# One core's decoder layer: eight modulation half-rows summed over the partitions by chained accumulating DMAs instead of by TensorE

## The chip, the core and the metric

The kernel runs on one core of one Trainium2 chip. The metric is the device time of one launch in microseconds (us), the median of three runs. TensorE is called PE, VectorE DVE, ScalarE ACT, GpSimd POOL and SyncE SP. POOL and SP each issue DMAs in the order of their own instruction stream; an instruction that waits holds up all that stands behind it on its engine.

## The reference, cut to what matters

One layer of a decoder on 512 tokens of width 1024, in float32. The modulation vectors come from one vector `c`:

```
cs  = silu(c)                                   # 1024
mod = cs @ w_ada + b_ada                        # 1024 x 6144
shift1, scale1, gate1, shift2, scale2, gate2 = split(mod, 6)
h    = rmsnorm(x, norm1_g) * (1 + scale1) + shift1
proj = h @ w_in                                 # queries, keys, values, gates ga and gd
merged = sigmoid(ga) * (swa(proj) @ w_branch_swa) + sigmoid(gd) * (diff(proj) @ w_branch_diff)
x  = x + gate1 * (merged @ w_out)
h2 = rmsnorm(x, norm2_g) * (1 + scale2) + shift2
x  = x + gate2 * conv_ffn(h2)
out = rmsnorm(x, final_g)
```

The change is about the last four of the six modulation vectors: gate1, shift2, scale2 and gate2. They are computed beside the two attentions and the merge, and are needed only after them.

## The kernel before, in words

Matrices are multiplied in float32 by splitting each operand into a high and a low half and adding three products (`mm3`: high x high, high x low, low x high); the halves of a weight are made by a cast on ACT and a subtraction on DVE (`split_pair`). Raw weights come over SP's queue into a ring of six buffers (`raw_tile`), so a load waits until the split that read its buffer is done.

From 57 us to 309 us PE runs through 288 steps of three 128x512 matmuls each: the projections of the four differential heads (`add_head`: pq, pk, pw), the gates of the windowed branch (`add_gate_a`: pga) with its branch product (pA), then the gates of the differential branch (`add_gate_d`: pgd) with theirs (`add_merge`: pB). Between the steps stand the small matmuls of the attentions. PE's order is the order in which the program is written: `fill(n)` emits n steps, and each call counts one tick. `after(n, fn)` has `fn` emitted n ticks later. The order on DVE, ACT, POOL and SP is set by a list scheduler with priorities; in the changed kernel POOL's order in this stretch, too, is the order of the program.

The four modulation vectors are 4 x 1024 numbers, kept as eight half-rows of 512 (named by vector and half: 00, 01, 10, 11, 20, 21, 30, 31). Every 8 ticks `ada_rows` loads 256 rows of `w_ada` for one half-row (tile `ra`) and DVE adds them, times `cs`, to a running sum of 128 partitions x 512 (tile `arow`); after four such turns, 32 ticks, the 128 partial sums of each of the 512 columns are ready. `ada_spread` then sums over the partitions: four float32 matmuls with a matrix of ones (tile `pr`), a copy on ACT to SBUF (tile `row`), and one DMA on POOL's queue into `mod_rows` in DRAM. Two running sums are alive at a time. Where `ada_spread` stands on PE is set by `flush("row")` at places written out by hand.

After the merge, gate1 is read back from `mod_rows` for all partitions (tile `g1b`) and multiplied into the rows of `w_out` (tile `wo`); shift2 and scale2 are read back as 16 x 128 (tile `m2`), and one transpose on PE (tile `pm2`) turns them for the second normalisation. Those reads stand on POOL's queue. POOL also takes the power -1/2 of the statistics of the differential heads (`rstd_start`, tile `r0`), for which DVE waits.

Of the kernel before, what the change touches and what calls it, by code (L numbers as in the profile page):

```python
# [11 lines left out]
ALU = mybir.AluOpType  # L12
# [45 lines left out]
def kernel(  # L58
# [52 lines left out]

    splits = []
# [376 lines left out]
    outa = [big.tile([P, 4, S], F32R, tag=f"out{g}", name=f"outa{g}") for g in "hl"]  # L489

    def evac(hi, lo, src, scale=None):
        if scale is None:
            nc.scalar.copy(hi, src)
            nc.vector.tensor_sub(lo, src, hi.bitcast(F32))
        else:
            nc.scalar.activation(hi, src, AF.Copy, scale=scale)
            return nc.vector.scalar_tensor_tensor(lo, src, scale, hi.bitcast(F32), ALU.mult, ALU.subtract)

# [33 lines left out]
    man = ExitStack()  # L532
    man.enter_context(tc.manual_schedule(engines={nc.tensor.engine}))
    units, loaded, later = [], [], []
    current, tick = [], [0]
# [30 lines left out]

    beside = {"row": [], "sum": [], "end": [], "norm": [], "turn": []}

    def after(n, fn):
        later.append([n, fn])  # L570
# [19 lines left out]
    def swa_scores(i, blocks):  # L590
# [26 lines left out]
        for n in blocks:  # L617
# [3 lines left out]
            for j in range(2):  # L621
                with tc.high_priority(offset=HP):
                    c.last = nc.vector.tensor_tensor_reduce(
                        c.sb[n][:, j, :w], sps[n // 2, j][:, n % 2, :w], dsw[:, 256 - w : 256], 1.0, -3e38, ALU.add, ALU.max,
                        c.mx[:, j, n : n + 1],
                    )

    def swa_softmax(i):
# [92 lines left out]

    maxima = []

    def diff_scores(*ss):
# [20 lines left out]
        for s, sps, w in ops:  # L745
# [3 lines left out]
            for m in range(2):  # L749
                st = ap.tile([P, w], F32, tag="st", bufs=ST, name=f"sd{h}_{n}_{m}")  # L750
                with tc.high_priority(offset=HP):
                    maxima.append(nc.vector.tensor_tensor_reduce(
                        st, sps[m], ddf[:, 512 - w : 512], 1.0, -3e38, ALU.add, ALU.max, mx[:, m : m + 1]
                    ))
# [4 lines left out]
    def diff_softmax(*ss):  # L759
        with tc.high_priority(offset=HP):  # L760
# [3 lines left out]
            for s in ss:  # L764
# [15 lines left out]
                behind.enter_context(tc.issue_after(last.ins))  # L780
            behind.close()

    def diff_transpose(s):
# [72 lines left out]
    def ada_rows():  # L856
# [5 lines left out]
        for (idx, hf, k), job in zip(todo, todo[ADA_AHEAD:] + [None] * ADA_AHEAD):  # L862
# [16 lines left out]
            if k == KT - 2:  # L879
                row = lambda idx=idx, hf=hf, ac=ac: ada_spread(idx, hf, ac)  # L880
                if group_ahead:
                    beside["row"].append(row)
                else:
                    after(ADA_LAG, row)
            yield

    spread = []


    def ada_spread(idx, hf, ac):  # L890
        pr = tbank(f"pr{idx}{hf}", (P, P))
        for g in range(4):
            gs = slice(32 * g, 32 * g + 32)
            nc.tensor.matmul(
                pr[gs], ones[:, gs], ac[:, g * P : (g + 1) * P], start=True, stop=True, tile_position=(0, 32 * g)
            )
        row = big.tile([P, P], F32, tag="g2b0", name=f"row{idx}{hf}")
        with tc.high_priority(offset=HP):
            spread.append(nc.scalar.copy(row, pr))  # L899
        nc.gpsimd.dma_start(  # L900
            mod_rows[idx, hf * S : (hf + 1) * S].rearrange("(g n) -> g n", g=4), row[0:P:32]
        )


    pair_w = {}

    def add_gate_a(j):
# [5 lines left out]
        def load():  # L913
            if j % 2 == 0:
# [6 lines left out]

                with tc.issue_after(spread[-1].ins) if j == 0 else ExitStack():
                    pair_w["a"] = split_pair(r, [P, 4, 2 * P], f"wba{j}")
            return pair_w["a"]

        def branch(wts):
            o = fbank(f"pA{j}")
            rhs = [[outa[b][:, k] for k in range(4)] for b in range(2)]
            yield from steps(o, wts, rhs, 4, cl=slice(j % 2 * P, j % 2 * P + P))
            nc.vector.scalar_tensor_tensor(ta[:, j], ta[:, j], 1.0, o, ALU.add, ALU.mult)  # L930

        units.append((lambda: load_cols(win, COL_GA + j * P, f"wga{j}"), gate))
        units.append((load, branch))

    group_ahead, sums = [1], {}
    pairs, firsts, scored, probs, aTs = {}, {}, {}, {}, {}
    ada = ada_rows()
    add_head(0)
    add_head(1)
    with tc.issue_after(last_mod.ins):  # L940
# [12 lines left out]
    for i in range(SWA_PAIRS):  # L953
        more = i + 1 < SWA_PAIRS
        fill(SWA_FILL[3])
        if more:
            flush("row")
            swa_scores(i + 1, range(NT))
# [10 lines left out]
        if i < 2:  # L969
            flush("row")  # L970
            swa_values(i)
        fill(SWA_FILL[7])
    while units or loaded or current:
        fill(1)
    flush("row")
    swa_values(2)
# [3 lines left out]
    ta = big.tile([P, KT, S], F32, tag="qa", name="ta")  # L980
    for j in range(2):
        add_gate_a(j)
    diff_scores(0, 1)
    diff_softmax(0, 1)
    fill(DIFF_FILL[0])
    for s in range(4 * DIFF_HEADS):
        h, n = divmod(s, NT)
        if s in (4, 8):
            add_head(h + 1)
        elif s == 12:  # L990
            add_gate_a(2)
            add_gate_a(3)
        ahead = s == 1
        fill(DIFF_FILL[1] - ahead)
        nxt = (s + 1, s + 2) if n % 2 and s < 15 else ()
        if nxt:
            flush("row")
            diff_scores(*nxt)
        if n == 3:
            with tc.issue_after(maxima[-1].ins):  # L1000
                flush("end")
# [7 lines left out]
        if n != 1:  # L1009
            diff_transpose(s)  # L1010
        if s == 13:
            group_ahead.clear()
        elif s > 13:
            flush("row")
        diff_softmax(*nxt)
        if n == 0 and h:
            diff_values(h - 1)
            fill(DIFF_FILL[3])
    for j in range(4, KT):
        add_gate_a(j)  # L1020
    fill(4)
    flush("norm")
    diff_values(DIFF_HEADS - 1)
    while units or loaded or current:
        fill(1)
# [16 lines left out]
    def add_gate_d(j):  # L1042
# [6 lines left out]
        units.append((lambda: load_cols(win, COL_GD + j * P, f"wgd{j}"), gate))  # L1049

    def add_merge(j):
        def load():
# [9 lines left out]
        def branch(wts):  # L1062
# [3 lines left out]
            td = tds[j]  # L1066
            nc.vector.scalar_tensor_tensor(td, td, 1.0, o, ALU.add, ALU.mult)
            nc.vector.tensor_add(td, td, ta[:, j])
            split(mgh[j], mgl[j], td)

        units.append((load, branch))

    for j in range(KT):
# [3 lines left out]
    add_merge(KT - 1)  # L1077
    while units or loaded or current or later:
        fill(1)
    for _ in ada:  # L1080
        fill(1)
    while later:
        fill(1)
    man.close()


    def brow(dst, src):
        nc.gpsimd.dma_start(dst, src.partition_broadcast(P))

# [8 lines left out]
    m2 = bp.tile([40, P], F32, name="m2")  # L1098
    nc.gpsimd.dma_start(m2[0:16, :], mod_rows[1:3].rearrange("r (a p) -> (r a) p", p=P))
    nc.gpsimd.dma_start(m2[16:32, :], b_ada[0, 3 * D : 5 * D].rearrange("(a p) -> a p", p=P))  # L1100
    nc.gpsimd.dma_start(m2[32:40, :], norm2_g[0].rearrange("(a p) -> a p", p=P))
    pm2 = tbank("pm2", (P, 40))
    nc.tensor.transpose(pm2, m2, ident[:40, :40])
    c2 = bp.tile([P, 40], F32, name="c2")
    nc.vector.tensor_copy(c2, pm2)
    nc.vector.tensor_add(c2[:, 0:16], c2[:, 0:16], c2[:, 16:32])
    s2c, a2c = c2[:, 0:8], c2[:, 8:16]
    nc.vector.scalar_tensor_tensor(a2c, a2c, 1.0, c2[:, 32:40], ALU.add, ALU.mult)
    nc.vector.tensor_scalar_mul(a2c, a2c, -0.5)

    x1 = big.tile([P, NT, D], F32, tag="qa", name="x1")
# [850 lines left out]
```

## Time and profile before

| | us |
|---|---|
| median of three runs | 691.83 (691.79 to 692.15) |
| the profiled execution | 692.45 |
| its span, first to last instruction | 690.5 |
| PE busy | 679.9 (98%) |
| DVE busy | 564.6 (82%) |
| ACT busy | 383.1 (55%) |
| POOL busy | 82.7 (12%) |

The granted clock of PE was 0.997 over the span. The span begins with the first normalisation and projection (to 57 us), goes on with the attentions and the merge (to 309 us), the product with `w_out` (to about 354 us), the gated MLP (to 683 us) and the last normalisation. Busy time of an engine does not count the issuing of DMAs, and idle time of an engine that nobody waits for costs nothing; so the table says little without the waits, which the prediction reads.

### The profile page before, as it was taken

The numbers are of one execution on the slowest core, as the hardware profiler recorded it, in microseconds if no ns is written. First come the engines' busy times: TensorE is split into PE (matmuls) and PEld (weight loads), VectorE is DVE, ScalarE is ACT, GpSimd is POOL, SyncE is SP. The second block draws the span as 40 slices with busy tenths as digits, with TensorE's granted clock in tenths as the row PEclk, the third lists the DMA queues.
The fourth block names the chain that finished last, engine by engine and source line by source line (L and its number), as shares of the span: only waits on it lengthen the run. The fifth ranks groups of instructions, "written<-read, shape, count | busy, mean of one in ns | idle before, by whom it ended". The sixth has DMA issues, their size and how long they took to land.

```text
span 690.5 us, 11249 instructions
## 1 busy us (share of the span) xinstructions
PE 679.9 (98%) x4203; PEld 592.7 (86%) x4203; DVE 564.6 (82%) x1073; ACT 383.1 (55%) x686; POOL 82.7 (12%) x100
## 2 busy tenths in 40 slices
PE   8999999999999999999999999999999999999995
PEld 5787877788888888888899999999999999888884
DVE  4889987878876775663589988888888999979997
ACT  6676775445542323332377756655555666656665
POOL 3000000000001000000030101112120002540300
PEclk9999999999999999999999999999999999999998
DMA  9995554444626882239635798777889747995903
GB/s 306 327 318 152 183 159 132 136 126 128 183 66 184 275 257 104 91 101 318 222 61 124 170 220 189 167 172 216 191 225 220 157 154 186 195 202 149 168 1 121
DMA packets 115926, 121.81 MB, mean 176 GB/s; under 512 B 4447, under 2 KB 93344, under 8 KB 115872
## 3 DMA queue, kind: packets, MB, share of 16 engines
q1 hardware_dynamic: 96958, 95.09, 43.7%
q0 software_dynamic: 18720, 25.73, 22.1%
q8 instruction: 33, 0.54, 0.3%
q10 hardware_dynamic: 194, 0.28, 0.1%
q14 instruction: 21, 0.17, 0.1%
HBM read 118.97 MB, written 2.11 MB: 175 GB/s over the span
## 4 chain that ended last, share of the span: by engine, by line
PE 95%; DMA 2%; DVE 1%; ACT 1%; issue 0%; SPq 0%; POOLq 0%; ACTq 0%
PE up L1291 32%; PE dc L1906 15%; PE a L388 3%; PE pga L125 2%; PE pgd L125 2%; PE oc L1347 2%; PE pga L127 2%; PE pga L126 2%; PE pgd L127 2%; PE oc L1351 2%; PE oc L1348 2%; PE pgd L126 2%; PE sd L132 1%; PE pq L125 1%; PE pw L125 1%; PE pA L125 1%
## 5 line engine op out<-in xcount | busy, mean ns | idle before, releaser
L1291 PE MATMUL up<-t,m_whi 128*128 128x256 f32 x512 | 93.1, 283 | 0.0
L1291 PEld LDWEIGHTS up<-t,m_whi 128*128 128x128 f32 x512 | 79.9, 192 | 0.0
L1291 PE MATMUL up<-t,m_wlo 128*128 128x256 f32 x256 | 72.5, 283 | 0.0
L1291 PE MATMUL up<-bl,p_whi 128*128 128x256 f32 x232 | 65.7, 283 | 0.0
L1291 PE MATMUL up<-bh,p_wlo 128*128 128x256 f32 x232 | 65.7, 283 | 0.0
L1291 PE MATMUL up<-bh,p_whi 128*128 128x256 f32 x232 | 65.7, 283 | 0.0
L1291 PEld LDWEIGHTS up<-t,m_wlo 128*128 128x128 f32 x256 | 49.2, 192 | 0.0
L878 DVE SCALAR_TENSOR_TENSOR arow<-ra,cs,arow 128x512 f32<-128x512 f32 x56 | 41.9, 748 | 8.1 <-DMA ra<-in_w_ada_dram 7.4
L1291 PEld LDWEIGHTS up<-bh,p_whi 128*128 128x128 f32 x232 | 44.5, 192 | 0.0
L1291 PEld LDWEIGHTS up<-bl,p_whi 128*128 128x128 f32 x232 | 44.5, 192 | 0.0
L1291 PEld LDWEIGHTS up<-bh,p_wlo 128*128 128x128 f32 x232 | 44.5, 192 | 0.0
L1200 POOL DMA_DIRECT2D s<-in_w_up_dram x21 | 27.0, 1362 | 140.5 <-DMA s<-in_w_up_dram 72.5
L1228 ACT CAST m_whi<-s 128x1024 fp32r<-128x1024 f32 x31 | 32.5, 1047 | 11.1 <-DVE s L1222 7.7
L1232 DVE TENSOR_TENSOR m_wlo<-s,m_whi 128x1024 fp32r<-128x1024 f32 x31 | 37.7, 1218 | 0.0
L1291 PE MATMUL up<-t,p_whi 128*128 128x256 f32 x176 | 32.2, 283 | 0.0
L188 POOL TENSOR_TENSOR r<-ms,mhalf 128x1 f32<-128x1 f32 (+1 forms) x16 | 13.1, 818 | 134.9 <-DVE ms L186 70.5
L900 POOL DMA_DIRECT2D mod_rows<-row x8 | 5.0, 630 | 194.2 <-ACT row L899 194.2
L1291 PEld LDWEIGHTS up<-t,p_whi 128*128 128x128 f32 x176 | 27.5, 192 | 0.0
L1298 ACT ACTIVATE gT<-a,cv 128x512 f32<-128x512 f32 x22 | 17.7, 813 | 16.9 <-DVE a L1333 15.8
L1228 ACT CAST p_whi<-wa 128x1024 fp32r<-128x1024 f32 x18 | 18.7, 1041 | 12.6 <-PE up L1291 12.6
L1232 DVE TENSOR_TENSOR p_wlo<-wa,p_whi 128x1024 fp32r<-128x1024 f32 x18 | 22.0, 1221 | 3.8 <-ACT p_whi L1228 3.8
L1291 PE MATMUL up<-t,p_wlo 128*128 128x256 f32 x88 | 24.9, 283 | 0.0
(491 smaller groups left out, 2062.4 us busy)
## 6 DMA issues: line engine op xcount, KB each, us to landing
ra<-in_w_ada_dram SPq DMA_DIRECT2D x32, 512.0 KB, 4.9
wa<-in_w_up_dram SPq DMA_DIRECT2D x22, 512.0 KB, 3.8
s<-in_w_up_dram SPq DMA_DIRECT2D x21, 512.0 KB, 4.5
s<-in_w_up_dram POOLq DMA_DIRECT2D x21, 512.0 KB, 6.8
adaw<-in_w_ada_dram SPq DMA_DIRECT2D x12, 512.0 KB, 7.2
w<-in_w_in_dram SPq DMA_DIRECT2D x12, 512.0 KB, 5.2
a<-in_w_up_dram SPq DMA_DIRECT2D x11, 512.0 KB, 4.8
b<-in_w_down_dram SPq DMA_DIRECT2D x10, 512.0 KB, 4.1
```

The lines of the kernel that those rows point to most:

```text
L125: nc.tensor.matmul(o, lh, rh, start=start, stop=False)
L126: nc.tensor.matmul(o, lh, rl, start=False, stop=False)
L127: nc.tensor.matmul(o, ll, rh, start=False, stop=stop)
L388: nc.tensor.matmul(acc6[i], lhs[:, i * P : (i + 1) * P], rhs[k], start=k == 0 and p == 0, stop=last and p == 2)
L878: nc.vector.scalar_tensor_tensor(ac, r[:, a], cc, ac, ALU.mult, ALU.add)
L1200: nc.gpsimd.dma_start(dst, upblock(*blk), accum_op=ALU.add)
L1228: nc.scalar.copy(W[J, name][0], R[J, SRC[name]])
L1232: nc.vector.tensor_sub(lo, R[J, SRC[name]], hi.bitcast(F32))
L1291: nc.tensor.matmul(o[u], w[:, k, cu], b[:, k], start=name in ("p1", "m5", "p2") and k == 0 and x == 0, stop=k == 3 and x == 2, skip_group_ ...
L1298: nc.scalar.activation(grow(j), av[J][:, u], AF.Identity, bias=cv[:, 66 + j : 67 + j], scale=cv[:, 44 + j : 45 + j])
L1347: nc.tensor.matmul(oacc[t][hf], a, wh[:, sl], start=k == 0, stop=False)
L1906: nc.tensor.matmul(bank2[u][:, sl], a[:, q, cu], b[:, q, sl], start=first_mm and x == 0, stop=last_mm and x == 2, skip_group_check=name no ...
```

## The change

The sum over the partitions leaves PE and ACT. `ada_sum` halves the running sum in place on POOL's queue: a DMA adds partitions 64 to 127 onto 0 to 63, the next 32 to 63 onto 0 to 31, and so on; after seven such accumulating DMAs partition 0 holds the half-row, and an eighth DMA writes it to `mod_rows`. Each of the eight reads what the one before has written, and waits for its landing. `HALVE` gives the ticks between them, and with that their places in POOL's order: 31 ticks from the last running sum to the eighth DMA. Three running sums are now alive at a time.

The running sums on DVE are held behind the latest of the operations collected in `paced` (the evacuations of PE's results), the splits of weights behind the latest softmax (`settled`). Units of PE's work are queued for the whole stretch at once and released by `due`, so that loads run ahead across the seams between stages. `m2` and `g1b` are read back over SP's queue, `m2` 44 ticks after the start of the merge, and `pm2` stands 12 ticks behind that in the merge, no longer behind it.

```diff
-ADA_LAG = 1
+HALVE = (1, 5, 5, 4, 4, 4, 4, 4)
-ROW_BEHIND = {0: -3, 4: -2}
+M2_LAG = (44, 56)
...
     def split_pair(raw, shape, name):
-        splits.append(split(hi, lo, raw))
+        with tc.issue_after(settled[-1].ins) if settled else ExitStack():
+            splits.append(split(hi, lo, raw))
...
-    man.enter_context(tc.manual_schedule(engines={nc.tensor.engine}))
+    man.enter_context(tc.manual_schedule(engines={nc.tensor.engine, nc.gpsimd.engine}))
...
-                if loaded:
+                if loaded and due[0]:
+                    due[0] -= 1
...
             if k == 0:
-                ac = big.tile([P, S], F32, tag=("sq2", "g2b1")[hf], name=f"arow{idx}{hf}")
-            if idx == 0 and hf == 1 and k in ROW_BEHIND:
-                hold = tc.issue_after(pairs[sorted(pairs)[ROW_BEHIND[k]]].divided.ins)
-            else:
-                hold = tc.issue_after(pairs[0].first.ins)
+                ac = big.tile([P, S], F32, tag=("sq2", "g2b1", "g2b0")[(2 * idx + hf) % 3], name=f"arow{idx}{hf}")
+            hold = tc.issue_after((paced[-1] if tick[0] > ADA_EASY else pairs[0].first).ins)
...
-    def ada_spread(idx, hf, ac):
-        pr = tbank(f"pr{idx}{hf}", (P, P))
-        for g in range(4):
-            gs = slice(32 * g, 32 * g + 32)
-            nc.tensor.matmul(
-                pr[gs], ones[:, gs], ac[:, g * P : (g + 1) * P], start=True, stop=True, tile_position=(0, 32 * g)
-            )
-        row = big.tile([P, P], F32, tag="g2b0", name=f"row{idx}{hf}")
-        with tc.high_priority(offset=HP):
-            spread.append(nc.scalar.copy(row, pr))
-        nc.gpsimd.dma_start(
-            mod_rows[idx, hf * S : (hf + 1) * S].rearrange("(g n) -> g n", g=4), row[0:P:32]
-        )
+    def ada_sum(idx, hf, ac):
+        def step(i):
+            n = P >> (i + 1)
+            if n:
+                nc.gpsimd.dma_start(ac[0:n], ac[n : 2 * n], accum_op=ALU.add)
+                after(HALVE[i + 1], lambda: step(i + 1))
+            else:
+                nc.gpsimd.dma_start(mod_rows[idx : idx + 1, hf * S : (hf + 1) * S], ac[0:1])
+
+        after(HALVE[0], lambda: step(0))
...
+    def load_m2():
+        nc.sync.dma_start(m2[0:16, :], mod_rows[1:3].rearrange("r (a p) -> (r a) p", p=P))
...
+    after(M2_LAG[0], load_m2)
+    after(M2_LAG[1], turn_m2)
...
-    brow(g1b, mod_rows[0])
-    brow(g1bias, b_ada[0, 2 * D : 3 * D])
-    nc.vector.tensor_add(g1b, g1b, g1bias)
-    nc.vector.tensor_scalar_mul(g1b, g1b, 0.5)
+    brow(g1b, mod_rows[0], nc.sync)
+    brow(g1bias, b_ada[0, 2 * D : 3 * D], nc.sync)
+    with tc.issue_after(merged[1][1].ins):
+        nc.vector.tensor_add(g1b, g1b, g1bias)
+        nc.vector.tensor_scalar_mul(g1b, g1b, 0.5)
```

Three places in the order show what moves. The first is POOL around half-rows 11, 20 and 21 (`row11` and `arow11` are of half-row 11; `r0` is the power of a head's statistics; `m2` and `g1b` are the reads back). Before:

```order
L188 TENSOR_TENSOR r0_2337<-ms_2335,mhalf_77 128x4
L900 DMA mod_rows_697<-row11_2350 4x128
L188 TENSOR_TENSOR r0_2497<-ms_2495,mhalf_77 128x4
L900 DMA mod_rows_697<-row20_2528 4x128
L1088 DMA g1b_3149<-mod_rows_697 128x1024
L1088 DMA xn0_3147<-in_b_ada_dram 128x1024
L1100 DMA m2_3154<-in_b_ada_dram 16x128
L1101 DMA m2_3154<-in_norm2_g_dram 8x128
L900 DMA mod_rows_697<-row21_2712 4x128
```

and in the changed kernel, from the end of half-row 11 to the end of half-row 20:

```order
L890 DMA arow11_2021<-arow11_2021 2x512
L890 DMA arow11_2021<-arow11_2021 1x16x32
L189 TENSOR_TENSOR r0_2496<-ms_2494,mhalf_77 128x4
L893 DMA mod_rows_697<-arow11_2021 16x1x32
L890 DMA arow20_2329<-arow20_2329 64x512
L890 DMA arow20_2329<-arow20_2329 32x512
L890 DMA arow20_2329<-arow20_2329 16x512
L890 DMA arow20_2329<-arow20_2329 8x512
L890 DMA arow20_2329<-arow20_2329 4x512
L890 DMA arow20_2329<-arow20_2329 2x512
L890 DMA arow20_2329<-arow20_2329 1x16x32
L893 DMA mod_rows_697<-arow20_2329 16x1x32
```

One DMA for each half-row has become eight in a chain, a power stands between two links of the chain of half-row 11, and the reads of `g1b` and `m2` have left POOL.

The second place is SP's queue in the merge (`wgd5` to `wgd7` are gate weights, `wbd4` and `wbd6` branch weights, `ra31_6` the last piece of `w_ada`, `wo0` the first rows of `w_out`). Before:

```order
L524 DMA wgd5_2913<-in_w_in_dram 128x8x128
L852 DMA ra31_6_2938<-in_w_ada_dram 128x2x512
L1055 DMA wbd4_2949<-in_w_branch_diff_dram 128x4x256
L524 DMA wgd6_2971<-in_w_in_dram 128x8x128
L524 DMA wgd7_3032<-in_w_in_dram 128x8x128
L1055 DMA wbd6_3064<-in_w_branch_diff_dram 128x4x256
L1125 DMA wo0_3183<-in_w_out_dram 128x1024
```

and now:

```order
L528 DMA wgd5_2912<-in_w_in_dram 128x8x128
L858 DMA ra31_6_2939<-in_w_ada_dram 128x2x512
L1044 DMA wbd4_2950<-in_w_branch_diff_dram 128x4x256
L1069 DMA m2_2675<-mod_rows_697 16x128
L528 DMA wgd6_2979<-in_w_in_dram 128x8x128
L528 DMA wgd7_3036<-in_w_in_dram 128x8x128
L1044 DMA wbd6_3069<-in_w_branch_diff_dram 128x4x256
L1124 DMA wo0_3183<-in_w_out_dram 128x1024
```

The read of `m2` from `mod_rows`, which waits for the eighth DMA of half-row 21, now stands ahead of the loads of the last two gates, of the last branch weights and of all of `w_out`. In the ring of six buffers, the load of `wo0` takes the buffer that `wgd5` leaves before, and the one that `wgd6` leaves now.

The third place is DVE in the merge (`wgd6_l` and `wbd4` are the low halves of weights, `tdall<-tdall,pB3` evacuates a branch product, `wo0<-wo0,g1b` scales rows of `w_out`). Before:

```order
L1126 TENSOR_TENSOR wo0_3183<-wo0_3183,g1b_3149 128x1024
L1126 TENSOR_TENSOR wo1_3190<-wo1_3190,g1b_3149 128x1024
L122 TENSOR_TENSOR wgd6_l_2974<-wgd6_2971,wgd6_h_2973 128x1024
L1067 SCALAR_TENSOR_TENSOR tdall_2675<-tdall_2675,pB2_2891 128x512
L1068 TENSOR_TENSOR tdall_2675<-tdall_2675,ta_1356 128x512
L122 TENSOR_TENSOR mg1l_2670<-tdall_2675,mg1h_2669 128x512
L1126 TENSOR_TENSOR wo2_3197<-wo2_3197,g1b_3149 128x1024
L122 TENSOR_TENSOR wgd7_l_3035<-wgd7_3032,wgd7_h_3034 128x1024
L1067 SCALAR_TENSOR_TENSOR tdall_2675<-tdall_2675,pB3_2954 128x512
L1068 TENSOR_TENSOR tdall_2675<-tdall_2675,ta_1356 128x512
L122 TENSOR_TENSOR wbd4_2951<-wbd4_2949,wbd4_2951 128x1024
```

and now:

```order
L123 TENSOR_TENSOR wgd6_l_2982<-wgd6_2979,wgd6_h_2981 128x1024
L123 TENSOR_TENSOR mg1l_2669<-tdall_2674,mg1h_2668 128x512
L123 TENSOR_TENSOR wgd7_l_3039<-wgd7_3036,wgd7_h_3038 128x1024
L1125 TENSOR_TENSOR wo0_3183<-wo0_3183,g1b_3160 128x1024
L1056 SCALAR_TENSOR_TENSOR tdall_2674<-tdall_2674,pB3_2955 128x512
L123 TENSOR_TENSOR wbd4_2952<-wbd4_2950,wbd4_2952 128x1024
```

In both, the scaling of `wo0` stands ahead of the low half of `wbd4`; now `wgd6_l` and `wgd7_l` stand ahead of the scaling too.

More of the change, by code (lines that the diff above doesn't have):

```diff
@@ L532 @@
     man = ExitStack()
-    man.enter_context(tc.manual_schedule(engines={nc.tensor.engine}))
-    units, loaded, later = [], [], []
+    man.enter_context(tc.manual_schedule(engines={nc.tensor.engine, nc.gpsimd.engine}))
+    units, loaded, later, due = [], [], [], [0]
     current, tick = [], [0]
@@ L565, in fill @@
                 next(ada, None)
-    beside = {"row": [], "sum": [], "end": [], "norm": [], "turn": []}
+    beside = {"sum": [], "end": [], "norm": [], "turn": []}
     def after(n, fn):
@@ L626, in swa_scores @@
                     )
+            paced.append(c.last)
     def swa_softmax(i):
@@ L781, in diff_softmax @@
             behind.close()
+            if ss:
+                settled.append(last)
     def diff_transpose(s):
@@ L929, in branch @@
             yield from steps(o, wts, rhs, 4, cl=slice(j % 2 * P, j % 2 * P + P))
-            nc.vector.scalar_tensor_tensor(ta[:, j], ta[:, j], 1.0, o, ALU.add, ALU.mult)
+            paced.append(nc.vector.scalar_tensor_tensor(ta[:, j], ta[:, j], 1.0, o, ALU.add, ALU.mult))
         units.append((lambda: load_cols(win, COL_GA + j * P, f"wga{j}"), gate))
         units.append((load, branch))
-    group_ahead, sums = [1], {}
+    sums = {}
     pairs, firsts, scored, probs, aTs = {}, {}, {}, {}, {}
     ada = ada_rows()
-    add_head(0)
-    add_head(1)
+    for h in range(2):
+        add_head(h)
+    for j in range(2):
+        add_gate_a(j)
+    for h in range(2, DIFF_HEADS):
+        add_head(h)
+    for j in range(2, KT):
+        add_gate_a(j)
+    due[0] = 6
     with tc.issue_after(last_mod.ins):
@@ L969 @@
         if i < 2:
-            flush("row")
             swa_values(i)
         fill(SWA_FILL[7])
-    while units or loaded or current:
+    while due[0] or current:
         fill(1)
-    flush("row")
     swa_values(2)
@@ L980 @@
     ta = big.tile([P, KT, S], F32, tag="qa", name="ta")
-    for j in range(2):
-        add_gate_a(j)
+    due[0] += 4
     diff_scores(0, 1)
@@ L988 @@
         if s in (4, 8):
[L989 removed]
+            due[0] += 3
         elif s == 12:
[L991 to L992 removed]
+            due[0] += 4
         ahead = s == 1
@@ L996 @@
         if nxt:
-            flush("row")
             diff_scores(*nxt)
         if n == 3:
-            with tc.issue_after(maxima[-1].ins):
+            with tc.issue_after(paced[-1].ins):
                 flush("end")
@@ L1018 @@
             fill(DIFF_FILL[3])
-    for j in range(4, KT):
-        add_gate_a(j)
+    due[0] += 2 * (KT - 4)
     fill(4)
@@ L1023 @@
     diff_values(DIFF_HEADS - 1)
-    while units or loaded or current:
+    while due[0] or current:
         fill(1)
@@ L1077 @@
     add_merge(KT - 1)
-    while units or loaded or current or later:
+    due[0] += len(units)
+    while due[0] or current or later:
         fill(1)
@@ L1084, with brow @@
     man.close()
-    def brow(dst, src):
-        nc.gpsimd.dma_start(dst, src.partition_broadcast(P))
+    settled.clear()
+    def brow(dst, src, q=nc.gpsimd):
+        q.dma_start(dst, src.partition_broadcast(P))
     TAIL = 3
```

55 lines of the change are left out of this document (23 added, 32 removed).

## The prediction

> **What bounds the kernel now.** I read the page first, then busy time by stage, then what PE waited for.
>
> ```profile
> span 690.5 us, 11249 instructions
> PE 679.9 (98%) x4203; PEld 592.7 (86%) x4203; DVE 564.6 (82%) x1073; ACT 383.1 (55%) x686; POOL 82.7 (12%) x100
> ```
>
> PE is busy for all but 10.6 us. The view of windows, over the stretch that the change touches (us, then busy us of PE, PEld, DVE, ACT and POOL with counts, granted clock, DMA share, GB/s):
>
> ```profile
> 110.00:170.00 60.00, 60.00 (x357) 48.05 (x354) 49.61 (x141) 31.26 (x76) 2.97 (x4) 1.00 0.50 148
> 170.00:243.00 73.00, 73.00 (x382) 60.06 (x381) 55.09 (x123) 31.12 (x60) 6.54 (x9) 1.00 0.56 174
> 243.00:310.00 67.00, 67.00 (x313) 53.99 (x312) 44.06 (x52) 21.01 (x30) 2.20 (x4) 1.00 0.42 135
> ```
>
> PE has no gap there at all, at full clock. The list of PE's waits starts with these (line waited at, what it waited for, us in total, times, longest):
>
> ```profile
> PE xt L411 <- DVE xn L406: 1.2, 2, 0.6
> PE a L177 <- POOL ones L136: 1.0, 1, 1.0
> ```
>
> Both belong to the head of the program. So this stretch lasts as long as PE's instructions do: what leaves PE is gained in full, and any new wait of PE is lost in full. DVE, ACT and POOL count only where PE comes to wait for them. Of DVE's 73 us from 170 to 243, 18 are idle.
>
> **What leaves PE.** The change removes eight `pr` groups. The chain of waits shows one a half-row (start, us):
>
> ```profile
> 200.87 0.35 PE pr L894 x8
> 220.93 0.35 PE pr L894 x8
> 243.74 0.36 PE pr L894 x8
> 266.09 0.36 PE pr L894 x8
> 288.43 0.36 PE pr L894 x8
> ```
>
> What such a group costs is read from the starts around it in PE's timeline:
>
> ```profile
> 287.82 0.39 PE L126 MATMUL pB<-outdB,wbd 128*128 128x512 f32 x1
> 288.05 0.39 PE L127 MATMUL pB<-outdA,wbd 128*128 128x512 f32 x1
> 288.36 0.42 PE L894 MATMUL pr<-arow,ones 128*32 128x128 f32 x8
> 288.72 0.50 PE L125 MATMUL pB<-outdA,wbd 128*128 128x512 f32 x1
> 289.06 0.39 PE L126 MATMUL pB<-outdB,wbd 128*128 128x512 f32 x1
> ```
>
> Two big matmuls start 0.23 apart; from 288.05 to 289.06 are 1.01, of which 0.46 would pass anyway: 0.55 for the group. Five stand so among big matmuls. The other three (before 110, before 170, and the one at 200.87) stand among small matmuls of the attentions, where I take the 0.35 of the chain. 5 x 0.55 + 3 x 0.35 = 3.8 us; bounds 8 x 0.36 = 2.9 and 8 x 0.55 = 4.4.
>
> **What costs nothing.** The eight row copies leave ACT, which is 55% busy. `pm2` moves within PE's order at the same price. The running sums stay 56 and 8 instructions; three buffers in place of two remove a wait of DVE:
>
> ```profile
> DVE arow L876 <- PE pr L894: 6.1, 3, 4.2
> L878 DVE SCALAR_TENSOR_TENSOR arow<-ra,cs,arow x56: 724/751/753, 61.1 to 253.8; 128x512 f32<-128x512 f32 x56
> ```
>
> PE never waited for that. Holding the sums behind evacuations, the splits behind the softmax, and the loads across seams are covered by DVE's idle time; if that cover is gone, one sum of 0.75 stands ahead of an evacuation PE waits for. I take 0, bounds -1 and +1.
>
> **The chain on POOL.** No chain of accumulating DMAs stands in the trace of before, so one link is bounded by its neighbours. These are POOL's writes of rows in three stretches of time (issue ns min/median/max, then us from issue to landing):
>
> ```profile
> L900 POOL DMA_DIRECT2D mod_rows<-row x3: 579/622/763, 109.5 to 167.9; - x3
> DMA to landing us min/median/max: 1.8/3.9/4.5
> L900 POOL DMA_DIRECT2D mod_rows<-row x2: 622/684/745, 201.9 to 221.9; - x2
> DMA to landing us min/median/max: 1.6/1.7/1.8
> L900 POOL DMA_DIRECT2D mod_rows<-row x3: 552/570/584, 244.7 to 289.4; - x3
> DMA to landing us min/median/max: 3.3/4.1/4.1
> ```
>
> Three of eight land in 1.6 to 1.8 us, five in 3.3 to 4.5, about as SP's loads are in flight or not; the mean is (1.8+3.9+4.5+1.6+1.8+3.3+4.1+4.1)/8 = 3.14. One step whose next instruction waited for a landing is there:
>
> ```profile
> 244.72 0.58 POOL L900 DMA_DIRECT2D mod_rows<-row  x1 [9.20 <-ACT row L899]
> 249.10 0.49 POOL L1099 DMA_DIRECT2D m<-mod_rows  x1 [3.80 <-DMA mod_rows<-row]
> ```
>
> From issue to issue it took 4.38, which is its landing, 4.1, and 0.28 more. So a step takes 1.9 (1.6 + 0.28) alone, 3.4 at the mean, 4.4 beside loads. The links are small but for the first three, of 64, 32 and 16 rows. For these I go by the page's list of queues:
>
> ```profile
> s<-in_w_up_dram POOLq DMA_DIRECT2D x21, 512.0 KB, 6.8
> ```
>
> These accumulating DMAs of 512 KB land in 6.8, some 3.2 above the rows' median; a quarter of that size adds 0.8, an eighth 0.4, a sixteenth 0.2: 1.4 a half-row. A half-row then holds POOL for 7 x 3.4 + 1.4 and 0.6 for the eighth's issue: 25.8 us. A new half-row comes every 22.8 (220.93 to 243.74) or 22.35. **That is the step on which the forecast rests: POOL falls behind by about 3 us a half-row** in the last four. `HALVE` helps nothing there: it sets places in the order, and a DMA whose predecessor is late waits.
>
> The Trainium skill, "DMA: Bandwidth & Descriptors", section on the anatomy of one DMA on the SWDGE (gpsimd) path, gives about 2.0 us fixed and bytes over 436,000 per us; by it eight links would take 16.6 us (an estimate) and keep pace. Three of the eight writes above agree; five do not. "SBUF — State Buffer", section "Who interferes with whom", speaks against the change instead: a VectorE instruction in a two-port mode shuts out GpSimd's making of descriptors. The issue times above, 552 to 763 ns, show at most 0.2 us of that here; with a whole `tensor_scalar` ahead of each link a step would be nearer 3.9.
>
> **Who waits for the chain.** Half-row 11's sum is complete when its `pr` stood, 200.87 less the 1.25 saved by then: 199.6. Three half-rows in a row on POOL: 11 to 225.4, 20 to 251.2, and 21 issues its eighth 25.2 later, at 276.4. It lands at 279.5; with no loads in flight the last two steps take 1.9, so 276.5. Call this landing L. There is no load in flight because SP stands at the read of `m2`, which waits for L, and behind it in SP's queue are the loads of `wgd6`, `wgd7`, `wbd6` and `wo0`. Before, SP had no such wait:
>
> ```profile
> 250.38 0.37 SPq L1055 DMA_DIRECT2D wbd<-in_w_branch_diff_dram  x1
> 251.51 3.40 SPq L524 DMA_DIRECT2D wgd<-in_w_in_dram  x2
> ```
>
> From L it goes on: `wgd6` is loaded, cast and split, which frees the buffer for `wo0`; `wo0` is loaded and scaled on DVE, and the low half of `wbd4` stands behind that scaling (and behind an evacuation) on DVE. Their rows, from the views of the tiles `wgd`, `wo`, `tdall` and `wbd`, and the two matmuls that mark the deadlines:
>
> ```profile
> DMA to landing us min/median/max: 3.9/4.4/4.9
> L121 ACT CAST wgd_h<-wgd x8: 1042/1055/1056, 230.7 to 278.0; 128x1024 fp32r<-128x1024 f32 x8
> L122 DVE TENSOR_TENSOR wgd_l<-wgd,wgd_h x8: 1217/1218/1226, 234.5 to 279.1; 128x1024 fp32r<-128x1024 f32 x8
> DMA to landing us min/median/max: 3.2/3.3/3.4
> L1126 DVE TENSOR_TENSOR wo<-wo,g1b x8: 1218/1226/1226, 267.2 to 303.8; 128x1024 f32<-128x1024 f32 x8
> L1067 DVE SCALAR_TENSOR_TENSOR tdall<-tdall,pB x8: 679/686/689, 255.9 to 308.8; 128x512 f32<-128x512 f32 x8
> L122 DVE TENSOR_TENSOR wbd<-wbd,wbd x4: 1214/1217/1219, 235.6 to 299.2; 128x1024 fp32r<-128x1024 f32 x4
> 280.79 0.39 PE L125 MATMUL pgd<-hThA,wgd_h 128*128 128x512 f32 x1
> 286.69 0.39 PE L127 MATMUL pB<-outdA,wbd 128*128 128x512 f32 x1
> ```
>
> 0.37 + 4.4 + 1.06 + 1.22 + 3.3 + 1.23 + 0.69 + 1.22 = 13.5 us from L to `wbd4`'s low half. PE's first use of that is the matmul at 286.69, less the 3.3 saved by then: 283.4. So PE waits from L = 270 on, and each us of L past it is a us of PE. (`pm2` now stands where 280.79 was, at 277.5; its read needs 4.4 at most, so it asks for L below 273, the weaker bound.) With L at 276.5 to 279.5 PE stands for 6.5 to 9.5; I take 8.0. What comes due later is moved by the same wait and not charged again; half-rows 30 and 31 end late too, which I put at 0 to 2 and take as 0.
>
> **The sum**, against the profiled execution, 692.45: less 3.8, plus 8.0, is 696.65. The median is 0.6 below that execution, so 696.0.
>
> **Rivals.** First, the other side: *the chain keeps pace.* L is 270 or earlier if three half-rows fit into 70.4 us, 22 steps and 5 us: a step of 2.97 or less. The landings of 1.6 to 1.8, and that links stay in SBUF where the rows above went to DRAM, speak for it; the five of 3.3 to 4.5 against. Then only the 3.8 counts: 691.83 - 3.8 = 688.0. Here also belongs what the skill's 2.0 us would give.
>
> Second, *stall and saving cancel*: a step near 3.1 to 3.25, a stall of 2.5 to 5.2, a time within 1.4 us of 691.83. These 1.4 us, 0.2%, are about the least that a measurement of this kernel tells from no change.
>
> Third, *steps near 4.4, and the powers held up too.* POOL's powers stand between links (before, this one ran as soon as its statistics were there):
>
> ```profile
> 217.91 1.03 POOL L188 TENSOR_TENSOR r<-ms,mhalf 128x4 f32<-128x4 f32 x1 [15.25 <-DVE ms L184]
> ```
>
> Now it stands behind the seventh link of half-row 11, whose seven steps of 4.4 and 1.4 end at 199.6 + 32.2 = 231.8, 14 us after it was wanted, and DVE's queue with the evacuations waits. At 3.9 a step, half-rows take 29.3, L is 291 (282 with free last steps) and the time 691.83 - 3.8 + 12 to 21: 700 to 709. At 4.4, three half-rows of 32.8 put L near 300 (286 with free last steps): 704 to 718.
>
> **How the numbers follow.** Forecast, 0.48: its own range 693.2 to 704. Pace kept, 0.36. Cancelled, 0.06. Powers held and over 705, 0.10. Faster 0.36, same 0.06, slower 0.58. The range goes from pace kept with 4.4 saved and up to 0.4 of the small gains, 687.0, to 705.0, a little over steps of 3.9 with free last links; 0.10 lie above, and about 0.04 below or between.
>
> **What would show it.** In the changed profile: no `pr`, PE busy about 3.8 less. Links of `arow` on POOL whose wait for the DMA before is near 3 us, with step times near 3.4. SP idle at the read of `m2` until after 270, and PE waiting, near 283, for the low half of `wbd4`, or for `pm2`. If the landings of the links have a median below 2.6, L is below 270 and the forecast falls to the first rival; above 3.6, it goes to the third. If PE stands where no row of `mod_rows` is behind it, the pacing of the sums or the splits has cost what I put at nothing.

## The result, and the profile after

| | before | after |
|---|---|---|
| median (us) | 691.22 (20 runs, 690.77 to 692.36) | 696.85 (20 runs, 691.87 to 704.70) |
| ratio to before | | 1.0088, 95% interval 1.0072 to 1.0104 |
| the profiled execution, its span | 692.45, 690.5 | 696.80, 695.0 |

The changed kernel is slower by 0.9%, 0.85 us above the predicted 696.0. One of its 20 runs, 704.70, counts as slow and is left out of the ratio; the other 19 still spread over 10 us, where the runs of before spread over 1.6. The page of the profile, span and busy times:

```profile
span 695.0 us, 11166 instructions
PE 679.5 (98%) x4139; PEld 592.9 (85%) x4139; DVE 564.7 (81%) x1073; ACT 381.6 (55%) x678; POOL 123.0 (18%) x151
```

PE's busy time hardly fell although `pr` is gone, so the page hides what happened. The view of windows (us, then busy us of PE, PEld, DVE, ACT and POOL, granted clock, DMA share, GB/s) shows the place:

```profile
110.00:170.00 60.00, 60.00 (x333) 48.52 (x330) 50.65 (x146) 30.43 (x74) 14.80 (x19) 1.00 0.60 161
170.00:243.00 73.00, 69.97 (x349) 57.52 (x348) 49.27 (x111) 28.75 (x55) 17.04 (x21) 0.98 0.60 173
243.00:310.00 67.00, 65.28 (x284) 52.79 (x283) 47.19 (x62) 20.19 (x26) 16.57 (x22) 1.00 0.61 177
310.00:360.00 50.00, 48.07 (x222) 39.59 (x222) 29.20 (x45) 18.49 (x31) 7.46 (x9) 1.00 0.67 211
```

PE, without a gap before, now stands in three of the stretches, and POOL's busy time from 170 to 310 has grown from 8.7 to 33.6. POOL's busy time does count the issuing of its DMAs, other than was said of the table of before: the issue of a link is 0.8 of it. The list of PE's waits (what waited, for what, us in total, times, longest):

```profile
PE pga L126 <- ACT ta L903: 2.2, 1, 2.2
PE oc L1347 <- DVE wo_l L123: 1.9, 1, 1.9
PE pB L128 <- DVE wbd L123: 1.7, 1, 1.7
PE od L127 <- DVE aTl L497: 0.8, 1, 0.8
```

That is 6.6 us in four waits; none stood in the list of before. Behind the first the granted clock fell as well (view of windows in steps of 5 us):

```profile
230.00:235.00 5.00, 2.78 (x10) 1.95 (x9) 2.84 (x4) 2.08 (x4) 0.76 (x1) 0.81 1.08 354
235.00:240.00 5.00, 5.00 (x21) 4.01 (x20) 2.23 (x3) 0.70 (x1) 1.60 (x2) 0.84 0.73 215
```

In windows of 1 us the clock reads 1.00 up to 233, then 0.57, 0.50, 0.50 and 0.72, and 1.00 again from 237: it was halved for about 3.4 us, which costs up to 1.7 on top of the wait.

What each wait cost with all that hangs on it is read against `no_links`, the changed kernel without the chain (below), whose PE runs the same instructions in the same order. The same matmul starts at 204.72 here and 204.94 there, then at 206.35 and 205.48, 237.24 and 232.40, 290.23 and 283.41, 342.96 and 333.93. So PE falls back by 1.1 at `od`, 4.0 at `pga`, 2.0 at `pB` and 2.2 at `oc`, 9.3 in all; behind that the distance no longer grows.

Now the cause, on POOL. All links (`L890`), and rows of POOL's timeline from the start of half-row 11 to the end of 21 (start, us, in brackets the idle time before and who ended it):

```profile
L890 POOL DMA_DIRECT2D arow<-arow x56: 757/789/1017, 107.6 to 324.4; - x56
DMA to landing us min/median/max: 1.8/3.1/5.9
...
195.38 0.81 POOL L890 DMA_DIRECT2D arow<-arow  x1 [7.96 <-DVE dls L780]
...
220.68 0.79 POOL L890 DMA_DIRECT2D arow<-arow  x1 [2.69 <-DMA arow<-arow]
221.23 1.32 POOL L189 TENSOR_TENSOR r<-ms,mhalf 128x4 f32<-128x4 f32 x1
...
272.94 0.79 POOL L890 DMA_DIRECT2D arow<-arow  x1 [1.97 <-DMA arow<-arow]
275.09 0.52 POOL L893 DMA_DIRECT2D mod_rows<-arow  x1 [1.37 <-DMA arow<-arow]
```

The links land in 3.1 at the median. Half-rows 11, 20 and 21 hold POOL from 195.38 to 275.09, and the power of the last head's rows stands behind the seventh link of 11: DVE's timeline shows the wait for it, 6.08, and SP's timeline the read of `m2`, which waits for half-row 21:

```profile
222.58 0.16 DVE L197 TENSOR_TENSOR rt<-r 128x4 f32<-128x4 f32 x1 [6.08 <-POOL r L189]
```

```profile
276.70 0.33 SPq L1069 DMA_DIRECT2D m<-mod_rows  x1
277.08 1.05 SPq L528 DMA_DIRECT2D wgd<-in_w_in_dram  x2
```

PE's timeline shows the wait for the low half of `wbd4` that the prediction named:

```profile
287.78 0.40 PE L127 MATMUL pB<-outdB,wbd 128*128 128x512 f32 x1
289.89 0.50 PE L128 MATMUL pB<-outdA,wbd 128*128 128x512 f32 x1 [1.72 <-DVE wbd L123]
```

The last wait, at `oc` in the product with `w_out`, the prediction had not named. On POOL, right behind half-row 31, stands the accumulating load of `s_t`, a weight of the gated MLP; on ACT its cast stands ahead of the last two casts of `wo` (POOL's, then ACT's timeline):

```profile
324.42 0.79 POOL L890 DMA_DIRECT2D arow<-arow  x1 [4.67 <-DMA arow<-arow]
...
330.19 1.33 POOL L1199 DMA_DIRECT2D s_t<-in_w_up_dram  x1
```

```profile
337.86 1.05 ACT L122 CAST m5w<-s_t 128x1024 fp32r<-128x1024 f32 x1 [8.02 <-DMA s_t<-in_w_up_dram]
338.81 2.00 ACT L122 CAST wo_h<-wo 128x1024 fp32r<-128x1024 f32 x2
```

Before, POOL issued that load 17 us earlier:

```profile
312.91 1.38 POOL L1200 DMA_DIRECT2D s_t<-in_w_up_dram  x1 [22.95 <-DVE mg3l L122]
```

### The profile page after: what moved, and what is told of

The parts are those of the page before. It is cut to its first block, busy times and chain, and to the rows that moved or that the text cites. A ratio compares the mean times of both kernels' runs of the same rounds, so it can differ in the third digit from the quotient of the medians.

```text
span 695.0 us, 11166 instructions
## 1 busy us (share of the span) xinstructions
PE 679.5 (98%) x4139; PEld 592.9 (85%) x4139; DVE 564.7 (81%) x1073; ACT 381.6 (55%) x678; POOL 123.0 (18%) x151
## 4 chain that ended last, share of the span: by engine, by line
PE 75%; DMA 17%; issue 4%; DVE 2%; POOL 1%; ACT 1%; SPq 0%; POOLq 0%; DVEq 0%; ACTq 0%
PE up L1290 32%; PE dc L1905 15%; DMA arow<-arow 14%; PE a L389 5%; PE pq L126 1%; PE pw L126 1%; PE sd L133 1%; DMA adaw<-in_w_ada_dram 1%; DMA s_t<-in_w_up_dram 1%; PE pk L126 1%; PE pq L128 1%; PE pq L127 1%; PE pw L128 1%; PE pw L127 1%; PE pk L128 1%
## 5 line engine op out<-in xcount | busy, mean ns | idle before, releaser
L890 POOL DMA_DIRECT2D arow<-arow x56 | 44.8, 800 | 236.7 <-DMA arow<-arow 132.5
L123 DVE TENSOR_TENSOR wgd_l<-wgd,wgd_h 128x1024 fp32r<-128x1024 f32 x8 | 9.8, 1224 | 20.8 <-ACT wgd_h L122 20.8
L189 POOL TENSOR_TENSOR r<-ms,mhalf 128x1 f32<-128x1 f32 (+1 forms) x16 | 13.2, 826 | 73.8 <-DVE ms L187 60.6
L1227 ACT CAST p_whi<-wa 128x1024 fp32r<-128x1024 f32 x18 | 18.7, 1042 | 12.6 <-PE up L1290 12.6
```

Source lines behind the costliest of these rows:

```text
L890: nc.gpsimd.dma_start(ac[0:n], ac[n : 2 * n], accum_op=ALU.add)
L1227: nc.scalar.copy(W[J, name][0], R[J, SRC[name]])
```

## The experiments

Two theories stood at the start. A: the chain of eight is late, and all that stands behind it on POOL, and SP behind its read, hands the delay to PE. B: the loss comes from the new timing of sums, splits and loads. All ratios are against runs of the kernel before on the same chip (691.3 to 691.6).

**The chain taken out** (`no_links`):

```
             if n:
-                nc.gpsimd.dma_start(ac[0:n], ac[n : 2 * n], accum_op=ALU.add)
                 after(HALVE[i + 1], lambda: step(i + 1))
```

> The changed kernel without the seven accumulating DMAs of each half-row; the eighth, the write, stays (so mod_rows holds partition 0's share only). Theory A (the chain is late: links of about 3.1 us hold POOL, the powers and, through the read of m2, SP): every stall of PE between 200 and 345 goes, and the time is 691.2 - 3.8 = 687.4, at most 688. Theory B (what was lost comes from the new timing of running sums, splits and loads across the seams): stalls near 230 and 288 stay, and the time is above 690.

687.64, against 691.38: 3.74 less, ratio 0.9943 (0.9929 to 0.9957). PE's list of waits has nothing left after 57 us:

```profile
PE a L178 <- POOL ones L137: 1.0, 1, 1.0
PE pc L254 <- POOL ident masks.py:199: 0.2, 1, 0.2
PE a L389 <- ACT hThA L373: 0.2, 1, 0.2
```

Theory B falls. Everything in the change but the chain is worth 3.74, and the chain costs 696.85 - 687.64 = 9.2; the four waits above, with what hangs on them, make it up.

**The loads beside the links taken out** (`no_ra`), with the running sums reading a tile that is in SBUF:

```
-                ready.append(ada_load(*job))
+                ready.append(None)
-                        nc.vector.tensor_scalar_mul(ac, r[:, a], cc)
+                        nc.vector.tensor_scalar_mul(ac, hTh[k].bitcast(F32), cc)
-                        nc.vector.scalar_tensor_tensor(ac, r[:, a], cc, ac, ALU.mult, ALU.add)
+                        nc.vector.scalar_tensor_tensor(ac, hTh[k].bitcast(F32), cc, ac, ALU.mult, ALU.add)
```

> The changed kernel without the 32 loads of w_ada of 512 KB each: the running sums read a tile that lies in SBUF instead, with the same instructions. If links are slow because SP's loads are in flight beside them: median landing 2.6 or less, a half-row below 22 us, no stall, 687 to 688. If a link is slow by itself: median 3.0 or more, half-row 21 late by as much as before, 692 or above.

688.57, ratio 0.9958 (0.9943 to 0.9973), and the links (view of the line):

```profile
L890 POOL DMA_DIRECT2D arow<-arow x56: 757/787/1015, 110.0 to 304.7; - x56
DMA to landing us min/median/max: 1.8/2.5/4.7
```

The median falls from 3.1 to 2.5, the longest from 5.9 to 4.7, and the last link stands at 304.7, no longer at 324.4; PE waits for nothing between 57 and 355. The write of half-row 21 is issued at 265.80, ahead of the 270 that the first rival asked for. So the loads in flight make a part of the link's price, enough to decide whether the chain keeps pace. A link does not fall to the shortest, 1.8, since other loads stay.

**`pr` alone taken out of the kernel before** (`no_pr`):

```
-        pr = tbank(f"pr{idx}{hf}", (P, P))
...
-            spread.append(nc.scalar.copy(row, pr))
+            spread.append(nc.scalar.copy(row, ac[:, 0:P]))
```

> The kernel before without the matmuls of pr: the copy on ACT reads the running sum itself, so mod_rows holds part of it unsummed; all else as before. The price of eight groups on PE: 3.8 (2.9 to 4.4), so 691.4 - 3.8 = 687.6, 687.0 to 688.5. If PE's place beside them was idle anyway: 691.

697.93, ratio 1.0101 (1.0084 to 1.0118): a miss, and no price of `pr`. the largest entry in PE's list is now a wait of the attentions for DVE:

```profile
PE td L789 <- DVE dls L775: 3.7, 2, 2.5
```

The scheduler had put DVE's instructions in another order, with running sums between those of the softmax (DVE's timeline):

```profile
139.47 0.16 DVE L775 RECIPROCAL dls<-dls 128x1 f32<-128x1 f32 x1
139.54 0.73 DVE L878 SCALAR_TENSOR_TENSOR arow<-ra,cs,arow 128x512 f32<-128x512 f32 x1
140.19 0.21 DVE L776 SCALAR_TENSOR_TENSOR dls<-dls,nlam 128x1 f32<-128x1 f32 x1
```

It suggests that the gain of `no_links` needs an order on DVE that lets PE run ahead, which the changed kernel has; whether its holds on the sums give it was not tried by itself. The price of `pr` is taken from `no_links`.

**One waiter at a time.** `m2_pool` moves the read of `m2` from SP to POOL:

```
-        nc.sync.dma_start(m2[0:16, :], mod_rows[1:3].rearrange("r (a p) -> (r a) p", p=P))
+        nc.gpsimd.dma_start(m2[0:16, :], mod_rows[1:3].rearrange("r (a p) -> (r a) p", p=P))
```

> The changed kernel with the read of m2 issued on POOL's queue instead of SP's; nothing else moves. Theory A: SP no longer stands until half-row 21 has landed, the waits at pB (about 2) and at oc (1.9) go, those at od and pga (1.3, and 2.6 with a dip of the clock behind it) stay: 696.9 - 4 = 693, with 692 to 694. If SP's wait is not what holds PE at pB: 696 to 698, and PE waits there as before.

698.94, ratio 1.0107 (1.0093 to 1.0121). A miss. The waits at `pB` and `oc` are gone, as expected, and the time is no shorter: the wait at `pga` is 3.8 in this execution, and now `pm2` waits too (POOL's, then PE's timeline).

```profile
278.73 0.52 POOL L893 DMA_DIRECT2D mod_rows<-arow  x1 [3.60 <-DMA arow<-arow]
279.24 0.85 POOL L890 DMA_DIRECT2D arow<-arow  x1
283.37 0.77 POOL L890 DMA_DIRECT2D arow<-arow  x1 [3.28 <-DMA arow<-arow]
283.89 0.75 POOL L1069 DMA_DIRECT2D m<-mod_rows  x1
```

```profile
287.46 0.22 PE L1073 MATMUL pm<-ident,m 40*128 40x40 f32 x1 [2.18 <-issue]
```

The read stands behind two links of half-row 30, and half-row 21 is itself 3.6 later.

The wait at `pga` shows one source of the changed kernel's scatter. In five kernels with the same `HALVE` half-row 11 begins between 195.4 and 196.0, and the power behind its seventh link starts, in the one profiled execution of each, at 217.76 (`row31_only`, below), 221.09 (`pow_only`, below), 221.23 (the changed kernel), 221.85 (`m2_late`, below) and 223.28 (`m2_pool`), and PE waits at `pga` for 0, 2.0, 2.2, 2.3 and 3.8. The links of a half-row do not take the same time twice, and PE pays for what is late.

`pow_ahead2` leaves SP as it is and moves the powers on POOL:

```
-HALVE = (1, 5, 5, 4, 4, 4, 4, 4)
+HALVE = (1, 11, 2, 2, 4, 8, 1, 1)
```

> The changed kernel with HALVE = (1, 11, 2, 2, 4, 8, 1, 1): the last two powers of the heads' statistics stand behind links 1 and 5 of half-row 11 on POOL, no longer behind links 2 and 7; the links themselves wait for their landings as ever. If the stalls add up: those at od and pga go, 696.9 - 4.8 = 692. Theory A says they do not add up: PE then comes to the merge 4 to 5 us earlier, and waits there for the same landing of half-row 21, so that one wait at pB or pm2 of 6 to 7 us takes the place of three, and the time stays at 695 to 697.5.

697.08, ratio 1.0080 (1.0066 to 1.0093): as theory A had it. The waits at `od` and `pga` are gone and have come back in the merge (PE's list of waits); with a granted clock of 0.50 from 290 to 295 behind them, PE again ends 9.6 later than in `no_links`:

```profile
PE pB L128 <- DVE wbd L123: 3.4, 1, 3.4
PE pm L1073 <- DMA m<-mod_rows: 1.8, 1, 1.8
```

`both2` is the sum of these two edits.

> Both edits together: m2 read on POOL, powers ahead of the late links. Theory A: no stall of PE is left between 57 and 310 us although the links are as slow as before (median landing near 3.1, half-rows ending late): 687.4 to 688.5, faster than the kernel before by 3 to 4. Theory B, or DMAs of the chain slowing SP's loads: stalls of 2 us or more stay, 690 or above.

700.11, ratio 1.0123 (1.0103 to 1.0144): a miss. PE waits 10.8 for `pm2` and 1.8 at `oc`, and the write of half-row 21 is issued at 283.45, where `pow_ahead2`, with the same order on POOL and SP standing at the read, issued it at 275.09. With SP free its loads go on beside the links.

So `pm2` has to move too. `both_late` adds `M2_LAG = (44, 92)` to `both2`, and `m2_late` the same to `m2_pool`.

> Powers ahead of the late links (HALVE as in pow_ahead2), m2 read on POOL, and the transpose pm2 36 ticks later (M2_LAG = (44, 92)), near the end of the merge, so that nothing of PE before 306 us needs half-row 21. Theory A (three waiters: the powers, SP behind the read, and pm2): no stall of PE is left although links stay as slow (median landing 3 to 3.7): 687.4 to 688.5. Rival: the late end of half-rows 30 and 31 (after 330) now shows in the first loads that the gated MLP wants from POOL's queue, up to 2 more: 689 to 690.

> m2 read on POOL and pm2 late, but HALVE as in the changed kernel: only the powers are held by links 2 and 7 of half-row 11. Nothing later covers them now. Theory A: the stalls at od (1.1) and pga (2.2 to 3.8, with 1.5 of lost clock behind it) show in full: 692 to 694. If the powers cost nothing by themselves: 687.5 to 688.5, as both_late.

700.64 (1.0106 to 1.0138) and 700.95 (1.0117 to 1.0159): both are misses. In `m2_late` PE waits at `oc` for 3.3 and 2.2, behind waits at `od` and `pga` as in the changed kernel. In `both_late` PE runs without a stall to 333 us, and then loses more than it had gained (PE's list of waits):

```profile
PE oc L1346 <- ACT wo_h L122: 8.1, 1, 8.1
PE oc L1347 <- DVE wo_l L123: 1.9, 1, 1.9
```

This is the load of `s_t` behind half-row 31, the wait that took 1.9 in the changed kernel, where the earlier waits had covered the rest. Theory C: waits in series behind one late queue, of which the last decides. To take it away, the third to eighth DMA of half-row 31 were issued behind that load, in three kernels: alone on the changed kernel (`row31_only`), on `m2_late` (`pow_only`), on `both_late` (`all_three`).

```
+            if (idx, hf, i) == (3, 1, 2):
+                last_row.append(ac)
...
+    with tc.issue_after(s_t1.ins):
+        ac = last_row[0]
+        for n in (16, 8, 4, 2, 1):
+            nc.gpsimd.dma_start(ac[0:n], ac[n : 2 * n], accum_op=ALU.add)
+        nc.gpsimd.dma_start(mod_rows[3:4, S : 2 * S], ac[0:1])
```

> The changed kernel with one edit: the third to eighth DMA of half-row 31 stand behind the accumulating load of s_t on POOL (s_t is a weight of the gated MLP, whose cast on ACT stands ahead of the last casts of wo). Theory C (four waiters in series: the powers, SP's read of m2, pm2, and s_t behind half-row 31; the last one ends last): the wait at oc (1.9) goes and the earlier ones stay: 696.9 - 1.9 = 695, 694 to 696.5. If s_t is not what ACT waits for: 697.

> m2 read on POOL, pm2 late, and half-row 31 behind s_t as in row31_only, but HALVE as in the changed kernel: of the waiters only the powers are left. Theory C: the stalls at od (1.1) and pga (2.2 to 3.8, and 1.5 of lost clock behind it) show in full and nothing else: 687.6 + 5 = 692.6, 691.5 to 694, against 701.0 of m2_late. If s_t was not what held oc there: 700 or above.

> All edits: powers ahead of the late links, m2 read on POOL and pm2 late, half-row 31 behind s_t. The links are as slow as before (median landing 3 to 3.6). Theory C: no stall of PE from 57 to 345, 687.5 to 689, faster than both kernels, against 700.6 of both_late. What could still cost: the powers of the second normalisation, wanted near 339, stand behind half-row 31 on POOL, which ends between 333 and 343: up to 4 more.

`row31_only` took 699.28 (1.0082 to 1.0133). Its profiled execution took 695.5, as expected, with no wait at `oc` and 4.0 at `pB`; the other five took 698 to 702, and what they waited for is in no trace: open. `pow_only` took 694.10 (1.0004 to 1.0049) and `all_three` 691.53 (0.9976 to 1.0018), both above what was expected. Still, the edit is worth 6.9 and 9.1 on these two: `s_t` was what decided there. The powers' own price is less sure. The medians differ by 694.10 - 691.53 = 2.6, but single runs of either kernel spread over 7 to 8 us; in the profiled execution of `pow_only` PE falls 4.6 behind `no_links` at `od` and `pga`, near the 5 expected. In `all_three` one wait is left between 57 us and the end, the one its expectation named (PE's list, then POOL's timeline); `pow_only` has it too, 2.0:

```profile
PE th L1396 <- DVE xn L1386: 2.5, 1, 2.5
```

```profile
341.38 0.52 POOL L1257 DMA_DIRECT2D mod_rows<-arow  x1 [2.46 <-DMA arow<-arow]
341.91 0.59 POOL L189 TENSOR_TENSOR r<-ms,mhalf 128x1 f32<-128x1 f32 x1
```

A power of the second normalisation stands behind half-row 31. `spread31` therefore spreads those six DMAs over POOL's gaps in the MLP, inside the loading of its weights:

```
+        with tc.issue_after(got.ins):
+            for n in {1: (16, 8), 2: (4,), 3: (2, 1)}.get(J, ()):
+                nc.gpsimd.dma_start(ac[0:n], ac[n : 2 * n], accum_op=ALU.add)
+            if J == 4:
+                nc.gpsimd.dma_start(mod_rows[3:4, S : 2 * S], ac[0:1])
```

> As all_three, but the last six DMAs of half-row 31 are spread over POOL's gaps in the gated MLP, two behind the first three accumulating loads of weights there, then one, two and one behind later ones, so that the four powers of the second normalisation and the loads stand ahead of them; the row is read back near 530. Theory C, now with five waiters: the wait at th (2.5 in all_three, on a power that stood behind half-row 31) goes, no stall of PE from 57 to 355, and the time is 687.6 to 689, 2.5 to 3.7 faster than the kernel before, with less spread from run to run. If links between the loads delay the weights of the MLP: new waits at up after 370, and 690 or above.

688.29, ratio 0.9949 (0.9936 to 0.9963): 3.2 faster than the kernel before and 8.6 than the changed one. Five of six runs lie between 687.94 and 688.54. The first execution, which is the profiled one, took 691.79: ahead of 50 us, where the chain has not begun, it falls 4.0 behind `no_links`, by a wait of 1.8 at `a` and a granted clock of 0.66 from 35 to 40, and from there to the end it loses nothing more. From 57 to 360 us its PE is busy without a gap (view of windows),

```profile
57.00:310.00 253.00, 253.00 (x1352) 205.55 (x1351) 197.37 (x477) 119.81 (x268) 49.13 (x62) 1.00 0.55 162
310.00:360.00 50.00, 50.00 (x254) 42.49 (x253) 28.49 (x51) 22.79 (x39) 8.58 (x10) 1.00 0.67 205
```

though its links are as slow as ever, 3.1 at the median.

## Why the prediction was right, and where it was not

- **What leaves PE: 3.8.** Right in size: 3.74 with the chain taken out, and since PE then waits for nothing after 57 us, sums, splits, loads across seams and ACT's copies cost nothing that shows. Not all of the 3.74 need be `pr`: of the 4.6 between the spans of the two profiled executions 1.15 lies in the head (the one `pcv` starts at 56.85 and 55.70), and 2.8 between there and the first `oc` (308.85 and 304.88), about the lower bound. The sum also took three groups as standing beside small matmuls where its rows have four (three before 170, and 200.87); by its own prices that makes 3.6.
- **The price of a link: a mean of 3.14 from eight writes.** Right: a median of 3.1 over 56 links. Half-rows 11 to 21 took 79.7 from the first issue to the last, 26.6 each. The Trainium skill, "DMA: Bandwidth & Descriptors", section on the anatomy of one DMA on the SWDGE (gpsimd) path, gave an estimate of about 16.6 for eight; half-rows 11, 20 and 21 took 27.4, 28.1 and 23.1, and even without the loads of `w_ada` the median link was 2.5.
- **POOL per half-row: 25.8, and L at 276.5 to 279.5.** Right in the result: the write at 275.09 had landed for the read at 276.70. Half-row 11 began at 195.38, 4.2 earlier than forecast, and the three took 79.7 where 76.8 was forecast.
- **13.5 from L to the low half of `wbd4`.** Right, step by step: from the read at 276.70 to PE's start at 289.89 are 13.2, with the cast of `wgd6` at 281.00, its low half at 282.08, the load of `wo0` at 283.33, its scaling at 286.88 and the low half of `wbd4` at 288.62.
- **8.0 lost at that matmul.** The rule was right, the place only in part. L at 276.70 asks for 6.7 by that rule, and PE does start this matmul 6.8 later than in `no_links`. But 4.8 of that it had lost before, at `od` and `pga`, since the powers had been held at steps of 3.1 already, and not only at 4.4, as the third rival had it. Where they are moved out of the way (`pow_ahead2`), PE waits 5.2 at `pB` and `pm2`. What a halved clock adds to a wait was not in the sum at all.
- **Half-rows 30 and 31: "0 to 2", taken as 0.** This is the step that failed. I did not follow POOL's queue past half-row 31 to the load of `s_t`. In the changed kernel the wait is 1.9 and costs 2.2. That the time came within 0.85 of the forecast is partly luck: this step was put 2.2 too low, and the 8.0 about 1.2 too high. The range from 687.0 to 705.0 would have held the first rival as well, so it is the rows that bear the argument out, and not that the time fell inside it. And it is the wait that ends last: with all the others gone the time was 700.64 (`both_late`), 13.0 above the 687.64 without a chain.
- **The first rival (pace kept, 688.0)** is what `no_ra` gives, 688.57, where the chain does keep pace; without the chain it is 687.64. The issues took 757 to 1017 ns, median 789, so at most 0.26 of waiting is in one; by the Trainium skill, "SBUF — State Buffer", section "Who interferes with whom", a VectorE instruction in a two-port mode would shut them out for its whole length, and no issue here shows that.

## What to carry to other kernels

An engine's queue that falls behind is not one wait but as many as there are things behind it, and they do not add up: taking away one only uncovers the next, until the last is found, so follow the queue to the end of the program before giving a price to any of them. Work that frees the busy engine by a chain of small dependent DMAs has to be priced at the landing under load, and kept out of the way of whatever else that queue owes: here 3.7 us were to be had, and 3.2 came in the one kernel here in which the powers of the heads and of the second normalisation, the read, the transpose and the load of `s_t` all stood clear of the chain. Which of these moves it could do without was tried for the powers and for half-row 31 alone.

## What the runs showed of the hardware

With SP's queue standing still POOL's links land sooner: half-row 21 took from 256.36 to 275.09, 18.7 us, with SP standing still from 263.5 on (`pow_ahead2`), and from 257.11 to 283.45, 26.3, with SP free (`both2`). In the changed kernel, where SP came to stand only at 268.6, it took 23.1.

What a stall costs beyond its length varies. Around the end of the 2.2 us of waiting at 233.37 the granted clock was halved for about 3.4 us, as the windows of 1 us above show. In the wait of 10.8 of `both2` it fell to 0.50 and was not back at full speed in the slice from 290 to 295, though the wait had ended at 287.51. A wait of 2.2 in `m2_pool` that ended at 287.46 left it at 1.00, and one of 2.0 in `pow_only` that ended at 233.04 brought it to 0.75. A row each of the views of windows of `both2`, `m2_pool` and `pow_only`:

```profile
290.00:295.00 5.00, 5.00 (x18) 4.03 (x17) 2.00 (x5) 0.00 (x0) 1.57 (x2) 0.76 0.38 111
```

```profile
285.00:290.00 5.00, 2.82 (x13) 2.12 (x12) 4.63 (x7) 1.67 (x2) 1.47 (x2) 1.00 0.57 148
```

```profile
235.00:240.00 5.00, 5.00 (x18) 3.98 (x17) 1.90 (x3) 0.35 (x1) 1.60 (x2) 0.75 0.75 230
```

The Trainium skill, "TensorE: Matmul & The Clock Gate", section "Part 1: The HAM clock gate", has the clock halved after an idle window of about 3.4 us; here waits of 2.0 and 2.2 were enough in one place and not in another, and what decides it no run here shows.
